# Modulation vectors as dot products along the rows, and small transfers on GpSimd's DMA queue

## The chip, the cores and the metric

One NeuronCore of one Trainium2 chip. The metric is device time in microseconds (us) from the first to the last instruction of one launch, with a little around it; the number given is the median of three runs. The engines are PE (TensorE matmul; PEld is its weight load), DVE (VectorE), ACT (ScalarE), POOL (GpSimd) and SP (SyncE). Each has its own instruction queue and runs it in order; SPq is SP's queue, which issues DMAs.

## The reference

Two transformer stacks on 256 tokens of width 1024, batch 1. The first has four layers of three sublayers each (SwiGLU, a mixer, SwiGLU); every sublayer is modulated by three vectors made from one conditioning row `c`:

```python
cond = silu(c)                                              # (1, 1024)
for i in range(4):
    mod = (cond @ w_mod[i] + b_mod[i]).reshape(-1, 3, 3, 1024)   # 9 vectors of 1024 for each layer
    ...
def _sublayer(x, fn, mod_j, g, b, weight):
    shift, scale, gate = mod_j[:, 0, None, :], mod_j[:, 1, None, :], mod_j[:, 2, None, :]
    y = fn(x * (1 + scale) + shift)
    return _layernorm(ALPHA * x + weight * gate * y, g, b)
```

The mixers are MLA attention (layers 0 and 3), differential attention (layer 1) and Mamba-2 (layer 2). The second stack is one block: a hybrid of dilated attention and retention, cross-attention to a memory of 256 tokens, and a SwiGLU. All is float32.

## The kernel before

Tokens lie in two tiles of 128 partitions (t = 0, 1). Each matrix product is done three times in a 12-bit split (high x high, high x low, low x high), so every weight tile that arrives is cast on ACT to its high part (`whi`, L219) and subtracted on DVE to its low part (`wlo`, L222). Weights come in pieces of 1 MB by SP's DMA queue into three buffers (`raw`, pool `rawp`), which the modulation weights share (`rawm`). The high and low parts live in a pool of `NW` = 21 buffers of 4 KB a partition.

A feed-forward sublayer (`ffn`, L598) has 11 blocks of 256 hidden units; a block is 48 matmuls of 512 columns into `hid` and 24 into `y`, with four transposes of `ac` between them. The mixers have hand-written step orders (`ORDER_MLA` and so on).

Work for later sublayers runs as background generators (`self.bg`): `tick` advances one by one step, at each block of an ffn (its `steps` argument spreads 32, 26 or 19 steps over the blocks) and at each "." of a mixer's order; `drain` runs what is left before the sublayer's result is normalized. The background makes the modulation vectors, each from four pieces of 1 MB:

- `mod_acc` (L357) loads a piece with the 1024 inputs over partitions and chunks and the 1024 outputs along the row, and adds up `acc[p, n]` over the eight chunks on DVE, with `cond` as a scalar of each partition. What remains is a sum over the 128 partitions.
- `mod_cols` (L375; 24 vectors, shift and scale) turns `acc` with eight 128x128 transposes on PE and sums each in a `tensor_reduce` on DVE, so that the vector comes out with features on partitions.
- `gate_row` (L410; 12 vectors) needs the vector as a row in all partitions (`gw`): it loads the bias broadcast, splits `acc` into high and low parts (ACT, DVE), and multiplies both halves with a matrix of ones on PE, four matmuls of 512 columns.

`post_ln` (L521) multiplies the sublayer's result by `gw`, then uses the rows `lng` and `lnb`. All DMAs, small ones too, are issued by SP.

The program is recorded in this order and then put in a queue for each engine by a list scheduler with a cost model; so an instruction's place in its queue is set before it runs, and it waits there for what it reads.

## Time and profile before

| | us |
|---|---|
| median of 3 runs (range) | 2570.22 (2568.35 to 2571.57) |
| the profiled execution, its span | 2567.9 |
| PE busy | 2497.5 |
| DVE busy | 2129.1 |
| ACT busy | 1286.9 |
| DMA, mean rate | 233 GB/s |

Only the span of the profiled execution is given (its own time with what lies around it is not); it is 2.3 us under the median of the three runs. Busy time counts a matmul until its modelled end, and matmuls overlap, so it is the distance from start to start that tells how fast PE goes through them.

### The profile page before, as it was taken

How to read it: one execution, taken by the hardware profiler on the slowest of the kernel's cores; microseconds unless marked ns; L12 is line 12 of the kernel's file. 1: busy time of each engine (PE TensorE's matmuls, PEld its weight loads, DVE VectorE, ACT ScalarE, POOL GpSimd, SP SyncE). 2: the span in 40 equal slices, each digit the busy share in tenths (PEclk: the TensorE clock that was granted, in tenths of full speed). 3: DMA queues.
4: the chain of work that ended last, by engine and by line, in shares of the span. 5: the costliest groups of instructions: out<-in, count | busy, mean ns of one | idle time of the engine just before them, and what ended most of it. 6: DMA issues, size and time to landing. Idle time of an engine off the chain costs nothing.

```text
span 2567.9 us, 34087 instructions
## 1 busy us (share of the span) xinstructions
PE 2497.5 (97%) x12252; PEld 2065.0 (80%) x12252; DVE 2129.1 (83%) x4847; ACT 1286.9 (50%) x2005; POOL 0.2 (0%) x4
## 2 busy tenths in 40 slices
PE   7999899999999999999999999999989999999998
PEld 6788688888887788888889778887878888788887
DVE  7888988879898988898989987698898856896754
ACT  3544474444446544544566554454446544555542
POOL 0000000000000000000000000000000000000000
PEclk9999999999999999999999999999999999999999
DMA  8888457848876388688742457658845754444552
GB/s 309 308 340 306 159 194 276 309 169 300 321 267 256 123 299 320 221 299 316 270 158 99 164 202 292 252 211 324 310 166 211 275 179 175 164 157 172 200 180 80
DMA packets 92297, 599.15 MB, mean 233 GB/s; under 512 B 12768, under 2 KB 14432, under 8 KB 24672
## 3 DMA queue, kind: packets, MB, share of 16 engines
q1 hardware_dynamic: 92128, 596.98, 63.5%
q8 instruction: 96, 1.57, 0.2%
q14 instruction: 73, 0.60, 0.1%
HBM read 593.79 MB, written 3.15 MB: 232 GB/s over the span
## 4 chain that ended last, share of the span: by engine, by line
PE 86%; DVE 7%; DMA 3%; ACT 2%; issue 1%; SPq 0%; DVEq 0%; ACTq 0%
PE tr L263 4%; PE y0q L640 3%; PE y0q L642 3%; PE y0q L641 3%; PE y1q L640 3%; PE y1q L642 3%; PE y1q L641 3%; DVE wlo L222 2%; PE hid0t L254 1%; PE hid6t L253 1%; PE hid9t L252 1%; PE hid6t L254 1%; PE hid9t L254 1%; PE hid6t L252 1%; PE hid5t L254 1%; PE hid9t L253 1%
## 5 line engine op out<-in xcount | busy, mean ns | idle before, releaser
L222 DVE TENSOR_TENSOR wlo<-raw,whi 128x384 fp32r<-128x384 f32 (+1 forms) x2385 | 1081.7, 505 | 145.8 <-ACT whi L219 76.0
L219 ACT ACTIVATE whi<-raw 128x1024 fp32r<-128x1024 f32 (+1 forms) x801 | 820.2, 1051 | 377.3 <-DMA raw<-in_ffn_w_in_dram 133.5
L371 DVE SCALAR_TENSOR_TENSOR acc<-rawm,cond,acc 128x1024 f32<-128x1024 f32 x252 | 322.9, 1281 | 13.2 <-DMA rawm<-in_w_mod_dram 8.0
L640 PE MATMUL y1q<-whi,ah 128*128 128x512 f32 x396 | 161.7, 408 | 1.7 <-ACT ah L625 1.7
L640 PE MATMUL y0q<-whi,ah 128*128 128x512 f32 x396 | 156.2, 394 | 0.7 <-ACT ah L625 0.2
L642 PE MATMUL y1q<-whi,al 128*128 128x512 f32 x396 | 156.4, 395 | 0.0
L641 PE MATMUL y0q<-wlo,ah 128*128 128x512 f32 x396 | 155.2, 392 | 0.0
L642 PE MATMUL y0q<-whi,al 128*128 128x512 f32 x396 | 155.2, 393 | 0.0
L641 PE MATMUL y1q<-wlo,ah 128*128 128x512 f32 x396 | 155.0, 391 | 0.0
L625 ACT ACTIVATE ah<-tr 128x256 fp32r<-128x256 f32 x198 | 74.7, 382 | 139.6 <-PE tr L263 136.7
L626 DVE TENSOR_TENSOR al<-tr,ah 128x256 fp32r<-128x256 f32 x198 | 82.0, 418 | 34.5 <-ACT ah L625 33.9
L640 PEld LDWEIGHTS y0q<-whi,ah 128*128 128x128 f32 x396 | 74.4, 188 | 17.1 <-ACT ah L625 2.6
L642 PEld LDWEIGHTS y1q<-whi,al 128*128 128x128 f32 x396 | 74.4, 188 | 15.7
L640 PEld LDWEIGHTS y1q<-whi,ah 128*128 128x128 f32 x396 | 74.5, 188 | 14.8 <-ACT ah L625 2.4
L642 PEld LDWEIGHTS y0q<-whi,al 128*128 128x128 f32 x396 | 74.3, 188 | 14.9 <-DVE al L626 0.2
L641 PEld LDWEIGHTS y0q<-wlo,ah 128*128 128x128 f32 x396 | 74.4, 188 | 14.5
L641 PEld LDWEIGHTS y1q<-wlo,ah 128*128 128x128 f32 x396 | 74.7, 189 | 13.2
L285 ACT ACTIVATE ev<-tr,B,G 128x128 f32<-128x128 f32 x192 | 72.9, 466 | 20.4 <-PE tr L263 20.3
L263 PEld LDWEIGHTS tr<-k_ident,ac 128*128 128x128 f32 x396 | 54.0, 140 | 29.6 <-DVE ac L616 3.0
L263 PE MATMUL tr<-k_ident,ac 128*128 128x128 f32 x396 | 74.5, 273 | 2.5 <-DVE ac L616 2.0
L295 DVE TENSOR_TENSOR tmp<-ev,tmp 128x512 fp32r<-128x512 f32 (+1 forms) x76 | 50.5, 664 | 12.7 <-ACT tmp L287 11.8
L252 PE MATMUL hid0t<-whi,tmp 128*128 128x512 f32 x144 | 56.4, 392 | 1.9 <-ACT tmp L287 1.9
(510 smaller groups left out, 6006.0 us busy)
## 6 DMA issues: line engine op xcount, KB each, us to landing
raw<-in_ffn_w_in_dram SPq DMA_DIRECT2D x176, 1024.0 KB, 4.9
rawm<-in_w_mod_dram SPq DMA_DIRECT2D x144, 1024.0 KB, 4.8
raw<-in_ffn_w_out_dram SPq DMA_DIRECT2D x88, 1024.0 KB, 5.0
raw<-in_w_gate_up_dram SPq DMA_DIRECT2D x22, 1024.0 KB, 4.7
raw<-in_w_in_dram SPq DMA_DIRECT2D x14, 1024.0 KB, 4.7
raw<-in_diff_w_in_dram SPq DMA_DIRECT2D x12, 1024.0 KB, 4.7
raw<-in_w_down_dram SPq DMA_DIRECT2D x11, 1024.0 KB, 4.7
raw<-in_w_kv_mem_dram SPq DMA_DIRECT2D x8, 1024.0 KB, 6.4
```

The source lines that it names most:

```text
L219: nc.scalar.activation(hi[:, q:e], s[:, q:e], AF.Copy)
L222: nc.vector.tensor_tensor(lo[:, q:e], s[:, q:e], hi[:, q:e].bitcast(F32), OP.subtract)
L252: nc.tensor.matmul(ps, xh, hi[:, off:off + n], start=first, stop=False)
L254: nc.tensor.matmul(ps, xl, hi[:, off:off + n], start=False, stop=last)
L263: self.nc.tensor.transpose(ps[:, j, :], src[:, j * P:(j + 1) * P], self.ident)
L285: nc.scalar.activation(src[:, j, :], ps[:, j, :], AF.Identity, scale=sc, bias=bcols[:, c + j:c + j + 1])
L371: nc.vector.scalar_tensor_tensor(o, src, sc, o, OP.mult, OP.add)
L625: nc.scalar.activation(ah, tr, AF.Copy)
L626: nc.vector.tensor_tensor(al, tr, ah.bitcast(F32), OP.subtract)
L640: nc.tensor.matmul(y[t][q], ah[:, k, :], hi[:, sl], start=f, stop=False)
L641: nc.tensor.matmul(y[t][q], ah[:, k, :], lo[:, sl], start=False, stop=False)
L642: nc.tensor.matmul(y[t][q], al[:, k, :], hi[:, sl], start=False, stop=l)
```

## The change

`w_mod` is laid out the other way: outputs on partitions, inputs along the row. `silu(c)` is kept as a row in all partitions (`condrow`, 4 KB a partition, for which `NW` goes from 21 to 20). A vector is then eight `scalar_tensor_tensor` instructions that multiply 1024 weights by `condrow` and add up along the row into one column of `pv` (`accum_out`); the product itself is written over the weights. Shift and scale are done with that. A gate is transposed once on PE (8x128), copied by ACT to `gs`, written to DRAM and read back broadcast to all partitions. The last two, and nearly all small transfers, go by GpSimd's queue. The number of background steps for each vector falls, and so do the ffn's `steps`.

```diff
-NR, NW, NT, NH = 3, 21, 12, 10
+NR, NW, NT, NH = 3, 20, 12, 10
...
     def bcast_row(self, dst, src, n):
         ap = bass.AP(tensor=src.tensor, offset=src.offset, ap=[[0, P], [1, n]])
-        self.nc.sync.dma_start(dst, ap)
+        self.nc.gpsimd.dma_start(dst, ap)
...
-    def mod_acc(self, i, s, m):
+    def mod_dot(self, i, s, m, pv):
         nc = self.nc
-        acc = self.tmp([P, 1024], name="acc")
         for u in range(4):
             raw = self.rawp.tile([P, 2048], F32, tag="raw", name=self.nm("rawm"))
             nc.sync.dma_start(raw, self.A["w_mod"][i, s * 3 + m, u])
             for j in range(2):
-                k = 2 * u + j
-                sc = self.cond[:, k:k + 1]
-                for q in range(0, 1024, ACH):
-                    src, o = raw[:, j * 1024 + q:j * 1024 + q + ACH], acc[:, q:q + ACH]
-                    if k == 0:
-                        nc.vector.tensor_scalar(o, src, sc, None, op0=OP.mult)
-                    else:
-                        nc.vector.scalar_tensor_tensor(o, src, sc, o, OP.mult, OP.add)
+                src = raw[:, j * 1024:(j + 1) * 1024]
+                nc.vector.scalar_tensor_tensor(src, src, 1.0, self.condrow, OP.mult, OP.mult,
+                                               accum_out=pv[:, 2 * u + j:2 * u + j + 1])
             yield
...
     def mod_cols(self, i, s, m):
         nc = self.nc
-        yield from self.mod_acc(i, s, m)
-        acc = self.acc
-        yield
         pv = self.small(8, "pv")
-        for a in range(0, 8, 4):
-            ps = self.transposes(acc[:, a * P:(a + 4) * P], 4)
-            nc.vector.tensor_reduce(pv[:, a:a + 4], ps, axis=AX.X, op=OP.add)
+        yield from self.mod_dot(i, s, m, pv)
...
     def gate_row(self, i, s):
         nc = self.nc
-        yield from self.mod_acc(i, s, 2)
-        acc = self.acc
+        pv = self.small(8, "pv")
+        yield from self.mod_dot(i, s, 2, pv)
+        nc.vector.tensor_tensor(pv, pv, self.bias_cols(i, s, 2), OP.add)
+        ps = self.bank("tr", "mod")
+        nc.tensor.transpose(ps[:8, :P], pv, self.ident)
+        gs = self.half([8, P], name="gs")
+        nc.scalar.activation(gs, ps[:8, :P], AF.Copy)
+        row = self.dr.tile([8, P], F32, name=self.nm("grow"))
+        nc.gpsimd.dma_start(row, gs)
         gw = self.tmp([P, D], name="gw")
-        self.bcast_row(gw, self.A["b_mod"][i, (s * 3 + 2) * D:(s * 3 + 3) * D], D)
-        for q in range(2):
-            sl = slice(q * 512, (q + 1) * 512)
-            ah, al = self.half([P, 512], F32R, "ah"), self.half([P, 512], F32R, "al")
-            nc.scalar.activation(ah, acc[:, sl], AF.Copy)
-            nc.vector.tensor_tensor(al, acc[:, sl], ah.bitcast(F32), OP.subtract)
-            yield
-            ps = self.bank("tr", "mod")
-            nc.tensor.matmul(ps, self.ones, ah, start=True, stop=False)
-            nc.tensor.matmul(ps, self.ones, al, start=False, stop=True)
-            nc.vector.tensor_tensor(gw[:, sl], ps, gw[:, sl], OP.add)
+        nc.gpsimd.dma_start(gw, row.rearrange("(o a) p -> o (a p)", o=1).to_broadcast([P, D]))
         self.gates[i, s] = gw
         yield
...
-        self.cond = c.tile([P, 8], F32, name="cond")
-        nc.scalar.activation(self.cond, cT, AF.Silu)
+        self.condrow = c.tile([P, D], F32, name="condrow")
+        self.bcast_row(self.condrow, A["crow"], D)
+        nc.scalar.activation(self.condrow, self.condrow, AF.Silu)
...
-                    self.ffn(xc, A["ffn_w_in"][f], A["ffn_w_out"][f], done, 32 if s == 0 else 26 if i + 1 in EARLY else 19)
+                    self.ffn(xc, A["ffn_w_in"][f], A["ffn_w_out"][f], done, 26 if s == 0 else 21 if i + 1 in EARLY else 16)
...
-    w = v["w_mod"].reshape(DEPTH, 4, 2, P, 9, D)
-    A["w_mod"] = np.ascontiguousarray(w.transpose(0, 4, 1, 3, 2, 5)).reshape(DEPTH, 9, 4, P, 2048)
+    A["crow"] = v["c"].reshape(D)
+    w = v["w_mod"].reshape(DEPTH, D, 9, 4, 2, P)
+    A["w_mod"] = np.ascontiguousarray(w.transpose(0, 2, 3, 5, 4, 1)).reshape(DEPTH, 9, 4, P, 2048)
```

Beside these, `nc.sync.dma_start` becomes `nc.gpsimd.dma_start` for the constants of `setup_late`, the positions and frequencies, `subg`, the Mamba constants, the writes of the memory's keys and values (`mk`, `mv`) and their reads in `cross` (`xk`, `xv`), the tables of `hybrid` and three norm gains: 89 DMAs in all leave by GpSimd's queue, and every 1 MB weight piece stays on SP's.

The schedule of each engine moves with it. On PE, in the first ffn, a shift or scale vector stood between the last `hid` matmul of block 3 and the first `y` matmul (`tr` is a PSUM bank, `acc` the sums):

```order
L252 MATMUL hid3t_225_1274<-whi_1209,tmp_608 128x512
L253 MATMUL hid3t_225_1274<-wlo_1210,tmp_608 128x512
L254 MATMUL hid3t_225_1274<-whi_1209,tmp_610 128x512
L263 MATMUL tr_1304<-k_ident,acc_1107 128x128 x4
L263 MATMUL tr_1310<-k_ident,acc_1107 128x128 x4
L640 MATMUL y1q_164_962<-whi_1013,ah_1183 128x512
L641 MATMUL y1q_164_962<-wlo_1014,ah_1183 128x512
```

After, the same place has only the two transposes of the block's own hidden units (`ac`):

```order
L252 MATMUL hid3t_218_1243<-whi_1178,tmp_577 128x512
L253 MATMUL hid3t_218_1243<-wlo_1179,tmp_577 128x512
L254 MATMUL hid3t_218_1243<-whi_1178,tmp_579 128x512
L263 MATMUL tr_1283<-k_ident,ac_1225 128x128 x2
L625 MATMUL y1q_157_931<-whi_982,ah_1152 128x512
L626 MATMUL y1q_157_931<-wlo_983,ah_1152 128x512
```

The eight transposes of `acc` are gone; nothing of the modulation stands on PE there. ACT's queue at the start of the kernel, before (`m`: the memory's tokens, `raw`: the first weights, `tmp` and `ev`: the memory's transposed tokens):

```order
L456 ACT_TABLE_LOAD
L456 ACTIVATE cond<-k_cT 128x8
L1143 ACTIVATE msq_103,ss_105<-m_85 128x1024
L1143 ACTIVATE msq_104,ss_106<-m_87 128x1024
L219 ACTIVATE whi_177<-raw_175 128x1024
L292 ACTIVATE tmp_99<-ev_142 128x4x128
```

And after:

```order
L445 ACT_TABLE_LOAD
L445 ACTIVATE condrow<-condrow 128x1024
L1128 ACTIVATE msq_98,ss_100<-m_83 128x1024
L1128 ACTIVATE msq_99,ss_101<-m_85 128x1024
L937 ACT_TABLE_LOAD
L937 ACTIVATE alog_11667<-alog_11667 128x32
L219 ACTIVATE whi_172<-raw_170 128x1024
L292 ACTIVATE tmp_94<-ev_137 128x4x128
```

The activation of the 1024 wide row `condrow` now stands ahead of the squares of the memory, and Mamba's `alog`, whose data come by GpSimd's queue, ahead of the first weight cast. That queue begins like this after (it had no DMA before):

```order
L332 DMA condrow<-in_crow_dram 128x1024
L1398 DMA pre_mix_g_690<-in_pre_mix_g_dram 128x8
L1398 DMA pre_mem_g_692<-in_pre_mem_g_dram 128x8
L1398 DMA pre_ffn_g_694<-in_pre_ffn_g_dram 128x8
L460 DMA k_tri<-in_tri_dram 128x128
L460 DMA k_slow<-in_slow_dram 128x128
L460 DMA k_ln_gT<-in_ln_gT_dram 128x96
L460 DMA k_ln_bT<-in_ln_bT_dram 128x96
L460 DMA k_mla_norm_g<-in_mla_norm_g_dram 128x10
L479 DMA posi<-in_positions_dram 128x2
L861 DMA subg<-in_diff_subln_g_dram 128x1
L332 DMA alog_11667<-in_ssm_a_log_dram 128x32
```

`posi` is the tenth DMA of that queue and `alog` the twelfth; `posi` and `subg` are read by DVE in the middle of the memory's first normalization (after `rv` of the second token tile).

## Rows read from the trace of the kernel before

**Rows 1.** Stretches: length, busy time and count by engine, PE clock, DMA share, GB/s.

```profile
20.00:45.00 25.00, 24.36 (x199) 23.69 (x198) 18.26 (x28) 8.10 (x10) 0.00 (x0) 0.99 0.95 365
...
1080.00:1275.00 195.00, 194.43 (x898) 159.28 (x897) 176.04 (x349) 88.39 (x132) 0.00 (x0) 1.00 0.80 296
1275.00:1490.00 215.00, 206.64 (x1337) 183.52 (x1336) 190.98 (x549) 128.02 (x183) 0.00 (x0) 0.98 0.38 134
```

**Rows 2.** PE's waits from 78 to 270 us: us, times, longest.

```profile
PE tr L263 <- DVE ac L616: 0.9, 1, 0.9
```

**Rows 3.** Timeline of PE at a shift or scale vector: start, us, what, count.

```profile
138.28 0.40 PE L254 MATMUL hid3t<-whi,tmp 128*128 128x512 f32 x1
138.52 1.04 PE L263 MATMUL tr<-k_ident,acc 128*128 128x128 f32 x8
139.31 0.48 PE L640 MATMUL y1q<-whi,ah 128*128 128x512 f32 x1
139.63 0.40 PE L641 MATMUL y1q<-wlo,ah 128*128 128x512 f32 x1
139.86 0.39 PE L642 MATMUL y1q<-whi,al 128*128 128x512 f32 x1
```

**Rows 4.** Timeline of PE at a gate: its first matmul, and the one after it.

```profile
190.78 0.39 PE L423 MATMUL mod<-ah,ones 128*128 128x512 f32 x1
...
191.71 0.39 PE L640 MATMUL y1q<-whi,ah 128*128 128x512 f32 x1
```

**Rows 5.** Groups by line: names, shapes, count, busy us, mean ns, idle before.

```profile
L371 DVE SCALAR_TENSOR_TENSOR acc<-rawm,cond,acc 128x1024 f32<-128x1024 f32 x252 | 322.9, 1281 | 13.2 <-DMA rawm<-in_w_mod_dram 8.0
...
L383 DVE TENSOR_REDUCE pv<-tr 128x4 f32<-128x512 f32 x48 | 31.2, 682 | 8.4 <-PE tr L263 8.4
...
L369 DVE TENSOR_SCALAR acc<-rawm,cond 128x1024 f32<-128x1024 f32 x36 | 26.9, 746 | 1.2 <-DMA rawm<-in_w_mod_dram 0.9
...
L425 DVE TENSOR_TENSOR gw<-mod,gw 128x512 f32<-128x512 f32 x24 | 16.3, 681 | 6.0 <-PE mod L424 6.0
L420 DVE TENSOR_TENSOR al<-acc,ah 128x512 fp32r<-128x512 f32 x24 | 16.2, 687 | 4.4 <-ACT ah L419 4.4
...
L574 ACT ACTIVATION_READ_ACCUMULATOR sq<-x 128x1 f32 x12 | 2.4, 200 | 0.0
```

**Rows 6.** Timeline of DVE in the first ffn: four multiply-adds in a row.

```profile
238.82 5.24 DVE L371 SCALAR_TENSOR_TENSOR acc<-rawm,cond,acc 128x1024 f32<-128x1024 f32 x4
```

**Rows 7.** Timeline of SP's queue: the first two DMA issues.

```profile
0.73 0.39 SPq L443 DMA_DIRECT2D k_cT<-in_cT_dram  x1
1.18 0.42 SPq L443 DMA_DIRECT2D k_ident<-in_ident_dram  x1
```

**Rows 8.** Tiles lnb (issue times, min/median/max) and gw (landing times).

```profile
L332 SPq DMA_DIRECT2D lnb<-in_ln_b_dram x12: 328/422/1425, 185.0 to 2039.5; - x12
...
DMA to landing us min/median/max: 3.4/5.8/8.2
```

**Rows 9.** DMA issues: count, KB each, us from issue to landing.

```profile
posi<-in_positions_dram SPq DMA_DIRECT2D x1, 1.0 KB, 3.9
alog<-in_ssm_a_log_dram SPq DMA_DIRECT2D x1, 16.0 KB, 5.3
```

**Rows 10.** Timelines of ACT, DVE and PE in the start stage.

```profile
5.78 1.06 ACT L1143 ACTIVATE msq<-m 128x1024 f32<-128x1024 f32 x1 [3.17 <-DMA m<-in_mem_dram]
...
11.16 1.06 ACT L219 ACTIVATE whi<-raw 128x1024 fp32r<-128x1024 f32 x1 [2.89 <-DMA raw<-in_w_kv_mem_dram]
...
8.31 0.15 DVE L314 TENSOR_SCALAR rv<-ss 128x1 f32<-128x1 f32 x1
...
70.56 0.73 PE L252 MATMUL pmv<-whi,tmp 128*128 128x512 f32 x2 [2.54 <-ACT whi L219]
```

**Rows 11.** Groups of ACT from 1275 to 1490 us, one table load of Mamba's.

```profile
L975 ACT ACT_TABLE_LOAD x1 | 1.3, 1283 | 0.0
```

**Rows 12.** Tile gw in the first MLA stage (270 to 392 us).

```profile
L425 DVE TENSOR_TENSOR gw<-mod,gw x2: 683/688/692, 352.9 to 362.8; 128x512 f32<-128x512 f32 x2
L528 DVE SCALAR_TENSOR_TENSOR r<-y0q,gw x2: 680/686/692, 358.3 to 363.5; 128x512 f32<-128x512 f32 x2
```

More of the change, by code (lines that the diff above doesn't have):

```diff
@@ L363, in mod_acc, with bias_cols @@
             for j in range(2):
-                k = 2 * u + j
-                sc = self.cond[:, k:k + 1]
-                for q in range(0, 1024, ACH):
-                    src, o = raw[:, j * 1024 + q:j * 1024 + q + ACH], acc[:, q:q + ACH]
-                    if k == 0:
-                        nc.vector.tensor_scalar(o, src, sc, None, op0=OP.mult)
-                    else:
-                        nc.vector.scalar_tensor_tensor(o, src, sc, o, OP.mult, OP.add)
+                src = raw[:, j * 1024:(j + 1) * 1024]
+                nc.vector.scalar_tensor_tensor(src, src, 1.0, self.condrow, OP.mult, OP.mult,
+                                               accum_out=pv[:, 2 * u + j:2 * u + j + 1])
             yield
-        self.acc = acc
+    def bias_cols(self, i, s, m):
+        o = (i * 9 + s * 3 + m) * 8
+        return self.bmod[:, o:o + 8]
     def mod_cols(self, i, s, m):
         nc = self.nc
-        yield from self.mod_acc(i, s, m)
-        acc = self.acc
-        yield
         pv = self.small(8, "pv")
-        for a in range(0, 8, 4):
-            ps = self.transposes(acc[:, a * P:(a + 4) * P], 4)
-            nc.vector.tensor_reduce(pv[:, a:a + 4], ps, axis=AX.X, op=OP.add)
-        b = self.bmod[:, (i * 9 + s * 3 + m) * 8:(i * 9 + s * 3 + m + 1) * 8]
+        yield from self.mod_dot(i, s, m, pv)
+        b = self.bias_cols(i, s, m)
         k = i * 3 + s - 1
@@ L454, in setup @@
         self.bmod = const("b_modT", [P, 288])
-        self.cond = c.tile([P, 8], F32, name="cond")
-        nc.scalar.activation(self.cond, cT, AF.Silu)
-        self.ones = c.tile([P, P], F32R, name="ones")
-        onesf = self.half([P, P], name="onesf")
-        nc.vector.memset(onesf, 1.0)
-        nc.vector.tensor_copy(self.ones, onesf)
+        self.condrow = c.tile([P, D], F32, name="condrow")
+        self.bcast_row(self.condrow, A["crow"], D)
+        nc.scalar.activation(self.condrow, self.condrow, AF.Silu)
     def setup_x(self):
@@ L956, in mamba @@
         cw = self.cst.tile([P, 24, 4], F32, name="cw")
-        nc.sync.dma_start(cw, A["ssm_conv_w"])
+        nc.gpsimd.dma_start(cw, A["ssm_conv_w"])
         cbb = self.cst.tile([P, 24], F32, name="cbb")
-        nc.sync.dma_start(cbb, A["ssm_conv_b"])
+        nc.gpsimd.dma_start(cbb, A["ssm_conv_b"])
         ng = self.cst.tile([P, 16], F32, name="ng")
-        nc.sync.dma_start(ng, A["ssm_norm_g"])
+        nc.gpsimd.dma_start(ng, A["ssm_norm_g"])
         dt, dta, ea, w, z, ys = {}, {}, {}, {}, {}, []
@@ L1205, in hybrid @@
                 K[name] = h[:, o:o + n]
[L1206 removed]
+                nc.gpsimd.dma_start(K[name], A[name])
                 o += n
         dec = self.tmp([P, 4, 256], name="dec")
[L1209 removed]
+        nc.gpsimd.dma_start(dec, A["decay"].rearrange("p (a b) -> p a b", a=4))
         db = self.half([P, P])
[L1211 removed]
+        nc.gpsimd.dma_start(db, A["dbias"])
         dbias = c.tile([P, P], BF16, name="dbias_b")
@@ L1412, in run @@
             g2[n] = self.cst.tile([P, 8], F32, name=n)
-            nc.sync.dma_start(g2[n], A[n])
+            nc.gpsimd.dma_start(g2[n], A[n])
         def grow(name):
```

27 lines of the change are left out of this document (11 added, 16 removed).

## The prediction

> **What bounds the kernel now.** I read the stretches by stage first. In an ffn with five modulation vectors (1080 to 1275 us) PE is busy 194.4 of 195 us, DVE 176.0, ACT 88.4, and the DMA engines 80% of the time at 296 GB/s [rows 1]. Then PE's waits: over the whole first ffn the longest line is 0.9 us [rows 2]. So in the ffns, which are most of the time, PE ends everything, and a PE instruction that disappears gives back its slot. Busy time is not the slot, since matmuls overlap: from start to start a matmul of 512 columns takes 139.86 - 139.63 = 0.23 us, not its 0.40 [rows 3]. Only the start stage and the first steps of each mixer are different: there PE waits for DVE and ACT, and what stands in front in their queues decides.
>
> **What leaves PE.** A shift or scale vector takes eight transposes: 139.31 - 138.52 = 0.79 us to the next matmul's start. That matmul then holds its slot 0.32 us (139.63 - 139.31) instead of 0.23, since its weight load is not hidden, and so the vector costs 0.79 + 0.09 = 0.88 us [rows 3]. 24 vectors: 21.1 us. A gate takes four matmuls from 190.78 to 191.71, 0.93 us [rows 4]; 12 gates: 11.2 us. What comes is one transpose for a gate: 0.79 / 8 = 0.10 us plus at most the 0.09, so 1.2 to 2.3 us for 12; I take 1.6. Net: 21.1 + 11.2 - 1.6 = 30.7 us off PE. Nearly all of it lies in ffns where PE is the bound; two vectors lie in the start stage and three gates in mixers (6 x 0.9 = under 5 us, of which part may have lain in PE's waits). I count 30.7 and put up to 3 us of doubt on it.
>
> **DVE.** Before, a vector was one first product and seven multiply-adds, 0.746 + 7 x 1.281 = 9.71 us; shift and scale add two sums over transposes (2 x 0.682, together 11.08), a gate two subtractions and two additions (2 x 0.687 + 2 x 0.681, together 12.45) [rows 5]. In all 24 x 11.08 + 12 x 12.45 = 415 us. After, it is 288 products with a sum along the row and twelve additions of eight columns, which I leave out. No row of before shows a DVE instruction with an accumulator. From below: the present ones stand 5.24 / 4 = 1.31 us apart, each reading the sum that the one before it wrote [rows 6]; the new ones need not wait for each other, so a product with its sum may come out at or somewhat under 1.28. From above: on ACT an accumulator's read is an instruction of its own of 0.200 us [rows 5]. I take 1.281 + 0.1: 288 x 1.38 = 398 us, 17 us less than before; with 0.2 it would be 427, 12 us more. Since DVE has 19 us to spare in the fullest ffn [rows 1], this is worth nothing by itself; PE hides it. The cover goes only if a product takes far longer (first rival).
>
> **ACT, the weight buffers and the steps.** 24 casts and the split leave ACT, which is idle half of the time. `NW` falls from 21 to 20: ten pairs of high and low parts stay, what goes is the one cast that ACT could make ahead of its partner, 1.06 us [rows 10], covered by ACT's idle half in an ffn; uncovered, it would be that 1.06 us for an ffn. In Mamba's stage ACT gets two more table loads (an `alog`-like change of table among Silu and Exp), 1.28 us each [rows 11]; ACT is busy 128 of 215 us there and PE 206.6 [rows 1], so I take 0.5 of the 2.6 us. The vector steps fall from 6 or 7 to 5, and the `steps` numbers with them, so the work is spread over the same blocks.
>
> **SP's queue** loses the small issues, and no longer waits for a buffer of `lng` or `gw` with weight pieces behind it. But PE hardly waits for weights in the ffns [rows 2]; I count nothing.
>
> **The start, where the change adds waits.** GpSimd issued no DMA before, so its issue is bounded by SP's: 1.18 - 0.73 = 0.45 us from issue to issue [rows 7], and 1.43 us for the longest issue [rows 8]. No row is nearer to the one or the other, so I take the middle, 0.95. (a) `condrow` is a 512 KB broadcast like `gw`, which lands 3.4 to 8.2 us after issue, median 5.8 [rows 8]: at 0.73 + 5.8 = 6.5, and its activation (1.06) holds ACT until 7.6, while the squares of the memory, queued behind it, began at 5.78 [rows 10]: 1.8 us lost (0 to 4.2). (b) DVE's cast of `posi`, the tenth issue, stands among the small steps after 8.31 [rows 10]: 0.73 + 9 x 0.95 + 3.9 [rows 9] = 13.2, against 8.4 + 1.8 = 10.2, so 3.0 more (0 to 7.3). (c) `alog`, the twelfth, stands ahead of the first weight cast, which began at 11.16 [rows 10]: 0.73 + 11 x 0.95 + 5.3 = 16.5 [rows 9], 5.4 late (0 to 10.6). (b) and (c) run side by side; the later counts: 5.4. Against that: shift and scale of the first sublayer are ready without PE and without the sums, so that the first inputs are scaled while PE still makes the memory's values, and ACT's weight casts no longer come late for PE, which waited 2.54 us for one [rows 10]. With two smaller ones of that kind I take 3.5 us back (0 to 4.7). Net at the start: +1.9 us, between -4 and +11.
>
> A rule bears on (a) to (c). The row: no small transfer lands under 3.9 us, and `condrow`'s like takes 5.8 [rows 8, 9]. The Trainium skill (DMA: Bandwidth & Descriptors, Anatomy of one DMA) has a fixed 2.0 us plus the bytes at 436 GB/s for a DMA from this queue, and little for making descriptors; by it `condrow` would land 3.2 us after issue, nothing would wait, and the sum would be some 5 us lower. No run here shows it yet.
>
> **The gate's detour.** In a mixer a gate used to be ready just in time: in the first MLA its second half was added at 362.8, and used from 363.5 [rows 12]. Now it is done two steps sooner (steps lie 362.8 - 352.9 = 9.9 us apart), at about 343, but then goes through two DMAs: 2 x (0.95 + 5.8) = 13.5, so 356.5, against a first use at 358.3 [rows 12]. It holds by 2 us; at the longest landing of 8.2 [rows 8] it comes 3 us late, in three mixers. I take 0, and up to 9 us in the range.
>
> **The sum,** against this execution's span of 2567.9: - 30.7 (PE) + 0.5 (tables) + 1.9 (start) = 2539.6. The median of the runs stands 2.3 above the span, so 2541.9. PE's few waits for the sums over transposes go too (1 to 2 us, not in the rows): 2540.
>
> **Rivals.**
> 1. *DVE becomes the bound, and the kernel slower.* If a product with its sum ran at half rate, 2.56 us: without modulation the ffn from 1080 has 176.0 - 4 x 11.08 - 12.45 = 119 us of DVE work; 40 products at 2.56 make it 221 against 195 before. Four such ffns: + 105 us, less what the rest gains (some 12): 2660. It decides from a product of 1.98 us on, where 4 x (119 + 40 x 1.98 - 195) eats the other 13 us. For it: no row shows the instruction. Against: with the same operands it now takes 1.28 [rows 5].
> 2. *The start and the gates cost more.* At 1.43 us an issue the start loses 10.6 - 3.5 = 7 instead of 1.9, and late gates add up to 9: 2546 to 2554. A mechanism that would bring it about: descriptors made in software while DVE, at work nine tenths of an ffn, holds them up. The Trainium skill (SBUF — State Buffer, Who interferes with whom) has this rule: DVE's fast two-port copies and scalar operations lock GpSimd out of its SBUF port. The change removes 36 such candidates (the 0.746 us products, against 1.28 for two inputs [rows 5]), which speaks for little of it.
> 3. *PE's time goes into waits for weights; no gain.* With 4.5 us less for an ffn the DMA rate has to rise from 296 to 303 GB/s; 365 GB/s are reached from 20 to 45 us [rows 1]. So against it. Time: about 2570.
> 4. *The start gains.* If GpSimd's small transfers land quickly, nothing is lost there and 3.5 to 4.7 is won, and the ffns lose their small stalls too: 2530 to 2535.
>
> **How the numbers follow.** Forecast with the start within its bounds (2533 to 2546): 0.60. Rival 4: 0.13. Rival 2: 0.15. Rival 3, or a new order of the queues that eats the gain: 0.06. Rival 1, or any other loss of that size: 0.06. The range takes the forecast with the bounds of the start, of the gates and of the tables, so rivals 2 and 4 with it: 2528 to 2556. About 0.2%, 5 us, is what a measurement of this kernel can tell from no change. Faster: 0.60 + 0.13 + 0.15 = 0.88; same 0.06; slower 0.06.
>
> **What would show it.** PE: no `tr` from `acc`, no `mod` of 512 columns; ffns of the first stack some 4 us (five vectors) to 3 us (three) shorter. DVE: `scalar_tensor_tensor` near 1.28 us with an accumulator read under 0.2; over 1.7 us, the forecast falls. Start: ACT's wait before `alog` and DVE's before `posi`, GpSimd's issues 0.5 to 1.4 us apart, the first ffn's first matmul moved by -4 to +11 us. Mixers: no wait of DVE for `gw`. PE waits growing in the ffns by tens of us would prove rival 3.

## The result: 0.65% slower, and where the time is in the profile after

| | kernel before | changed kernel |
|---|---|---|
| median of four runs (range), us (of the kernel before, the three ahead and one more) | 2569.28 (2565.57 to 2571.57) | 2584.62 (2575.30 to 2589.02) |
| ratio to the kernel before, 95% interval | | 1.0065 (1.0044 to 1.0085) |
| span of the profiled execution, us | 2567.9 | 2573.4 |
| mean granted clock of PE | 0.992 | 0.989 |
| PE busy, DVE busy, us | 2497.5, 2129.1 | 2475.2, 2072.1 |

The prediction was 2540 us, in a range of 2528 to 2556, with a chance of 0.88 for faster. The changed kernel is slower. Run again beside the experiments, it took 2580.73 us where the kernel before took 2566.95 (ratio 1.0055, interval 1.0038 to 1.0072). The profiled execution was the fastest of the four, so what the trace shows (5.5 us) is the smaller part of the loss of 15.3.

I cut both traces at the first matmul of each stage and compared stage by stage. First the ffns whose modulation changed, of the changed kernel: the first row has four vectors (two shifts or scales, two gates), the second five (four and one), as the ffn in [rows 1], the third three (two and one); the last line sums all eight ffns. Columns: stretch, length, busy time and count of PE, PE's weight loads, DVE, ACT and POOL, granted clock, share of the DMA engines, GB/s.

```profile
898.90:1087.60 188.70, 188.23 (x854) 153.71 (x854) 158.23 (x358) 91.45 (x134) 3.16 (x6) 1.00 0.78 284
1087.60:1277.60 190.00, 188.80 (x855) 153.95 (x854) 167.27 (x376) 88.79 (x134) 3.16 (x6) 1.00 0.82 301
...
388.40:577.20 188.80, 188.20 (x854) 153.88 (x852) 148.61 (x338) 90.72 (x132) 2.10 (x4) 1.00 0.72 256
...
sum 1519.30, PE 1506.98 PEld 1230.35 DVE 1247.45 ACT 718.98 POOL 25.48; mean PE 188.37 PEld 153.79 DVE 155.93 ACT 89.87 POOL 3.19
```

The same three ffns, and the same sum, of the kernel before:

```profile
884.40:1077.30 192.90, 192.36 (x876) 157.01 (x877) 166.05 (x336) 94.11 (x138) 0.00 (x0) 1.00 0.76 279
1077.30:1270.50 193.20, 192.77 (x889) 157.84 (x888) 174.24 (x347) 89.19 (x134) 0.00 (x0) 1.00 0.79 296
...
377.20:568.30 191.10, 190.47 (x873) 156.44 (x872) 154.02 (x321) 92.20 (x134) 0.00 (x0) 1.00 0.69 253
...
sum 1542.20, PE 1532.26 PEld 1255.12 DVE 1301.85 ACT 729.38 POOL 0.00; mean PE 191.53 PEld 156.89 DVE 162.73 ACT 91.17 POOL 0.00
```

So the ffns did much of what was forecast: 4.2 us less with four vectors, 3.2 with five, 2.3 with three, and 22.9 us less in all. The four ffns with five vectors are uneven: 5.0, 0.5, 3.2 and 4.8 us less. Now the start, the first MLA, diff, Mamba and the second MLA of the changed kernel:

```profile
0.00:89.60 89.60, 59.87 (x321) 51.76 (x322) 59.65 (x142) 41.27 (x61) 12.80 (x27) 0.92 0.78 289
279.50:388.40 108.90, 94.89 (x518) 79.24 (x518) 90.05 (x236) 59.55 (x123) 2.11 (x4) 0.95 0.49 173
770.00:898.90 128.90, 121.70 (x619) 96.00 (x618) 107.08 (x274) 72.24 (x150) 2.10 (x4) 0.96 0.49 177
1277.60:1505.00 227.40, 217.51 (x1384) 191.82 (x1383) 201.11 (x566) 135.93 (x195) 0.00 (x0) 0.98 0.40 139
1885.30:1992.80 107.50, 94.72 (x519) 79.04 (x519) 89.99 (x236) 59.34 (x123) 2.10 (x4) 0.97 0.50 175
```

and of the kernel before:

```profile
0.00:78.40 78.40, 58.82 (x337) 51.25 (x338) 57.91 (x115) 36.40 (x57) 0.20 (x4) 0.93 0.82 310
273.30:377.20 103.90, 95.97 (x520) 79.90 (x521) 91.73 (x231) 61.03 (x125) 0.00 (x0) 0.97 0.51 182
761.60:884.40 122.80, 117.98 (x621) 93.60 (x619) 108.69 (x269) 71.77 (x150) 0.00 (x0) 1.00 0.51 185
1270.50:1496.00 225.50, 216.99 (x1386) 191.90 (x1385) 201.48 (x567) 135.09 (x199) 0.00 (x0) 0.98 0.40 141
1883.60:1987.90 104.30, 96.23 (x521) 80.31 (x522) 90.87 (x229) 60.07 (x124) 0.00 (x0) 0.97 0.50 180
```

The start is 11.2 us longer, the first MLA 5.0, diff 6.1, Mamba 1.9, the second MLA 3.2. Together that is 27.4 us, more than the ffns give. The clock column is part of it: a stretch's length times (1 - clock) is the most that PE can have lost at its lower level, since time in which it waits anyway counts in it. By these rows that is 16.2 us before (5.5, 3.1, 0, 4.5, 3.1) and 25.5 us after (7.2, 5.4, 5.2, 4.5, 3.2), 9.3 us more. The columns of PE say the same from the other side: the time in which PE is not busy grew by 24.7 us in these stages, and its busy time by 2.7, although by the prediction's prices some 4.2 us of its work had gone from them. So the clock's part is some 7 us, an estimate, and at most 9.3 by these rounded rows; most of the loss is PE's waits.

**The start.** Rows of ACT, of DVE, of SP's queue and of PE in the changed kernel, each engine for itself in order of time; a bracket says how long the engine stood idle before and what ended that.

```profile
7.59 1.06 ACT L445 ACTIVATE condrow<-condrow 128x1024 f32<-128x1024 f32 x1 [5.58 <-DMA condrow<-in_crow_dram]
8.56 1.04 ACT L1128 ACTIVATE msq<-m 128x1024 f32<-128x1024 f32 x1
...
15.74 0.23 ACT L937 ACTIVATE alog<-alog 128x32 f32<-128x32 f32 x1 [3.71 <-DMA alog<-in_ssm_a_log_dram]
15.88 1.04 ACT L219 ACTIVATE whi<-raw 128x1024 fp32r<-128x1024 f32 x1
...
13.82 0.17 DVE L481 CAST posf<-posi 128x2 f32<-128x2 int32 x1 [2.77 <-DMA posi<-in_positions_dram]
...
31.88 12.45 SPq L361 DMA_DIRECT2D rawm<-in_w_mod_dram  x4
46.57 3.02 SPq L211 DMA_DIRECT2D raw<-in_w_kv_mem_dram  x2
...
54.02 0.73 PE L252 MATMUL pmv<-whi,tmp 128*128 128x512 f32 x2 [4.57 <-ACT whi L219]
...
74.62 1.22 PE L252 MATMUL pmv<-whi,tmp 128*128 128x512 f32 x2 [7.08 <-ACT whi L219]
```

The squares, the cast of `posi` and the first weight cast are late as in [rows 10] against these: 5.78 became 8.56, and 11.16 became 15.88. But two waits have grown as well. Four pieces of vector rows stand in SP's queue ahead of the third weights of the memory (issued at 46.57; in the kernel before two stood there, and these weights were issued at 37.57), and PE waits 4.57 us for them. In the kernel before it waited here too, but less:

```profile
47.56 0.57 PE L253 MATMUL pmv<-wlo,tmp 128*128 128x512 f32 x1 [3.09 <-DVE wlo L222]
```

Then ACT scales the first inputs before it casts the fourth weights, and PE waits 7.08 us, where [rows 10] has 2.54.

**The opening of the first MLA.** DVE in the changed kernel; `rs` and `rt` are the steps of the root that PE's next transposes (of `cn`) need:

```profile
289.72 0.21 DVE L320 TENSOR_SCALAR rs<-rt,rs 128x1 f32<-128x1 f32 x1
289.84 1.21 DVE L364 SCALAR_TENSOR_TENSOR rawm<-rawm,condrow 128x1024 f32<-128x1024 f32 x1
...
290.98 0.27 DVE L319 TENSOR_SCALAR rt<-rh,rs 128x1 f32<-128x1 f32 x1
291.17 1.22 DVE L364 SCALAR_TENSOR_TENSOR rawm<-rawm,condrow 128x1024 f32<-128x1024 f32 x1
...
292.62 0.48 DVE L753 TENSOR_SCALAR cn<-pa,rs 128x256 f32<-128x256 f32 x1
...
295.05 1.23 DVE L364 SCALAR_TENSOR_TENSOR rawm<-rawm,condrow 128x1024 f32<-128x1024 f32 x1 [1.46 <-DMA rawm<-in_w_mod_dram]
```

Two products stand in the middle of that chain; in the kernel before the first piece of the vector came on DVE only after it, at 296.2 (there the chain's end was at 284.51). It is in the order of the instructions, and could have been seen before the run. PE waits 5.53 us there, where the kernel before has 3.67. Then the third product stands ahead of the last step of `kr` (296.20), which PE transposes next; it waits 1.46 us for its own rows to land and takes 1.2, and PE waits a second time, 2.60 us. Over the whole execution PE's line for this wait (put down to `rv`, the step behind) was `0.6, 1, 0.6` (us, times, longest) before and is now

```profile
PE tr L263 <- DVE rv L314: 4.1, 2, 2.6
```

What these two waits grew by is 4.5 of the 5.0 us of the first MLA. At the opening of diff three products stand in such a chain (777.77 to 781.63), and PE waits 3.17 us, where the longest wait there was 1.21.

What the clock does behind these openings, first in the MLA, then during and behind the wait in diff (stretches of the changed kernel, columns as above):

```profile
293.00:297.00 4.00, 1.24 (x4) 0.63 (x5) 2.54 (x15) 0.18 (x1) 0.00 (x0) 0.50 0.59 202
...
781.00:785.00 4.00, 0.83 (x5) 0.39 (x4) 4.00 (x8) 2.60 (x3) 0.00 (x0) 1.00 1.00 414
785.00:790.00 5.00, 4.25 (x17) 3.28 (x17) 5.00 (x9) 4.38 (x11) 0.00 (x0) 0.52 0.38 161
```

The clock falls to its lower level of 1.2 GHz (0.50 and, with some time at the upper level, 0.52). In the MLA PE is in its second wait for most of that stretch, so little is lost in it; in diff it is busy 4.25 of 5 us again, and works at half speed.

### The profile page after: what moved, and what is told of

It is laid out like the page before. It is cut to its first block, busy times and chain, and to the rows that moved or that the text cites. A ratio compares the mean times of both kernels' runs of the same rounds, so it can differ in the third digit from the quotient of the medians.

```text
span 2573.4 us, 34066 instructions
## 1 busy us (share of the span) xinstructions
PE 2475.2 (96%) x12024; PEld 2041.0 (79%) x12024; DVE 2072.1 (81%) x5049; ACT 1281.1 (50%) x1995; POOL 47.8 (2%) x93
## 4 chain that ended last, share of the span: by engine, by line
PE 81%; DVE 10%; DMA 4%; ACT 4%; issue 2%; DVEq 0%; POOL 0%; ACTq 0%; SPq 0%; POOLq 0%
DVE wlo L222 3%; PE tr L263 3%; PE y0q L625 3%; PE y0q L627 3%; PE y0q L626 3%; PE y1q L625 3%; PE y1q L626 3%; PE y1q L627 3%; DMA rawm<-in_w_mod_dram 2%; PE hid9t L252 1%; PE hid8t L253 1%; PE hid9t L254 1%; PE hid2t L252 1%; PE hid4t L252 1%; PE hid4t L254 1%
## 5 line engine op out<-in xcount | busy, mean ns | idle before, releaser
L364 DVE SCALAR_TENSOR_TENSOR rawm<-rawm,condrow 128x1024 f32<-128x1024 f32 x288 | 342.3, 1222 | 27.5 <-DMA rawm<-in_w_mod_dram 26.7
L626 PEld LDWEIGHTS y1q<-wlo,ah 128*128 128x128 f32 x396 | 74.7, 189 | 13.2
L295 DVE TENSOR_TENSOR tmp<-ev,tmp 128x512 fp32r<-128x512 f32 (+1 forms) x76 | 50.9, 670 | 17.8 <-ACT tmp L287 16.6
```

Source lines behind the costliest of these rows:

```text
L364: nc.vector.scalar_tensor_tensor(src, src, 1.0, self.condrow, OP.mult, OP.mult, accum_out=pv[:, 2 * u + j:2 * u + j + 1])
L626: nc.tensor.matmul(y[t][q], ah[:, k, :], lo[:, sl], start=False, stop=False)
```

## The experiments

Times are medians; the ratio is to the kernel before, run on the same chip beside each group. The groups ran on different chips, so the ratios compare them, and a difference in us between groups is only about right. Theory A says that the loss is made by the order: products that stand in the chains which open a layer, and the vectors' rows ahead of the weights at the start. Theory B says that GpSimd's DMA queue makes everything late. Theory C came later: a wait of PE costs a second time, by the clock.

**The changed kernel again, as the reference.**

> The changed kernel itself, beside the three that follow, as their reference on the same chip. If its loss belongs to the kernel and not to one chip: ratio to the kernel before 1.0065 within its interval of 1.0044 to 1.0085, so 2580 to 2589 where the kernel before takes 2567 to 2569. If it comes out at 2576, the three runs that came to 2576 gained nothing.

2580.73 us, ratio 1.0055 (1.0038 to 1.0072). The loss belongs to the kernel. So a run below that comes to 2576 has gained 4 to 5 us, not 8 to 9. The intervals of the runs hold, start_held, dots_sp and start_sp_b overlap this one, so what each of these four gained is read from its stages; those of the other runs on the changed kernel lie clear of it. In the trace of this run (span 2582.8) the loss is larger than in the first: the ffns sum to 1525.6 us, only 16.6 less than before, and the start is 13.2 us longer.

**Products behind the chain.**

```diff
+                with self.tc.issue_after(self.mark):
                     nc.vector.scalar_tensor_tensor(src, src, 1.0, self.condrow, OP.mult, OP.mult, ...
```

> The changed kernel with one edge: no modulation product is placed on DVE ahead of the last transposed half of the layer's input. In the two MLAs and in diff that puts the products back behind the short root-of-variance chain that PE waits for; everything else stays. Theory A (products in the chains, and the start): MLA0 back from 108.9 to about 104 us, diff from 128.8 to 123, MLA1 from 107.5 to 104.5, so 12 to 14 us less than the changed kernel's median of 2584.6: about 2572, ratio to the kernel before about 1.001. Theory B (the second DMA queue is slow everywhere): the chains are not the cause, the time stays at 2584.

2575.78 us, ratio 1.0039 (1.0023 to 1.0055). Diff came back as forecast, to 123.6 us. The MLAs did not: 109.4 and 110.2 us. (The traced execution took 2581.04 us, 5 over the median.) The wait at the opening fell from 5.53 to 3.50 us (3.67 in the kernel before), and the second one of 2.60 is gone, but new ones came at the query projections; PE, SP's queue and DVE in this run:

```profile
313.99 0.47 PE L252 MATMUL pq<-whi,tmp 128*128 128x512 f32 x1 [2.16 <-DVE vt L793]
317.48 0.80 PE L253 MATMUL pq<-wlo,tmp 128*128 128x512 f32 x1 [3.03 <-DVE wlo L222]
...
305.59 2.43 SPq L211 DMA_DIRECT2D raw<-in_mla_w_q_dram  x2
...
313.94 1.22 DVE L365 SCALAR_TENSOR_TENSOR rawm<-rawm,condrow 128x1024 f32<-128x1024 f32 x1
...
316.88 1.36 DVE L222 TENSOR_TENSOR wlo<-raw,whi 128x384 fp32r<-128x384 f32 x3
```

The rows already stood in two of the three raw buffers, and stayed there until the products were done (the second began at 304.33, its sum was read at 305.48), so the query weights were issued at 305.59 instead of 292.42. That alone is not the cause: the kernel before issued them at 298.73, 25 us into its stage as here 26, and its waits at this place were 1.19 and 0.37 us. What differs is the place of the next two products: they stand from 313.94 to 316.35 ahead of the `wlo` that PE waits 3.03 us for. So the edit freed one short chain, and the products came to stand in the next.

**The start's order put right, GpSimd's queue kept.**

```diff
-        nc.scalar.activation(self.condrow, self.condrow, AF.Silu)
...
+        with self.tc.issue_after(squares):
+            nc.scalar.activation(self.condrow, self.condrow, AF.Silu)
...
+        with self.tc.issue_after(self.mark_d):
             nc.vector.tensor_copy(pf, pi)
...
+        with self.tc.issue_after(self.mark_a):
             nc.scalar.activation(alog, alog, AF.Exp)
```

> The changed kernel with the start's order put right and nothing else: Silu of condrow behind both squares of the memory on ACT, the casts of posi and subg behind the memory's last transposed half on DVE, alog's Exp behind the memory's values on ACT. All transfers stay on GpSimd's queue. Theory A: PE's first matmul back from 15.6 to about 10 us, so 5.6 us less than the changed kernel: about 2579; PE's wait of 7 us for the last weights of the memory's values (ACT scales the first inputs before them) stays. Theory B: as little as 0 to 2 us less, because the queue itself delays what follows.

2575.96 us, ratio 1.0036 (1.0023 to 1.0049). PE's first matmul came at 11.53 us instead of 15.56, and the first ffn at 84.6 instead of 89.6, so 5.0 of the 11.2 us are this order. The waits for the third and fourth weights stayed, at 6.88 (4.57 in the changed kernel) and 6.51 us.

**All small transfers on SP's queue again.**

```diff
-        nc.gpsimd.dma_start(row, gs)
+        nc.sync.dma_start(row, gs)
```

(and so at all twenty places)

> The changed kernel with all its small transfers on SP's queue again, gate rows too; the row products stay. Products in the chains of MLA and diff stand where they stand in the changed kernel. Theory A: only the start changes, since the scheduler then puts posi, subg and alog late: 5 to 8 us less than the changed kernel, 2577 to 2580. Theory B (the queue): all that was lost comes back, 2545 or less.

2576.73 us, ratio 1.0041 (1.0025 to 1.0056). The first ffn starts at 83.2 us; the first MLA still takes 110.3 and diff 128.2. Theory B falls: without GpSimd's queue only the start gets better. PE's first matmul is back at 9.38 us there, and its waits for the third and fourth weights are still 7.81 and 6.51 us.

**The queue alone, on the kernel before.**

```diff
-        self.nc.sync.dma_start(dst, ap)
+        self.nc.gpsimd.dma_start(dst, ap)
```

(and so at all small transfers)

> The kernel before with its small transfers on GpSimd's queue (constants, rows, the memory's keys and values out and in, lng, lnb, gw) and nothing else: modulation by multiply-add, sums over transposes, gates by the matrix of ones. Theory A: the start loses 3 to 5 us by posi and alog, the rest nothing: 2573, ratio 1.0015. Theory B: most of the loss of 45 us against the sum of the parts is here: 2585 or more.

2573.65 us, ratio 1.0026 (1.0017 to 1.0035): 6.6 us more, where theory A had 3 to 5 and theory B 18 or more. The start accounts for them: the first ffn comes at 85.2 us instead of 78.4. The other stages are 3.2 us shorter to 2.3 us longer, with no sign of theory B's 18.

**Another order at the start.**

```diff
-L0 . . L1 . K0 . . . . K1 L2 . R . . V2 X Q E0 E1 L3 V3
+L0 . . L1 K0 . L2 . K1 . L3 . R . . V2 X . . . Q E0 E1 V3
```

(with the one-time transfers on SP's queue)

> The changed kernel with another start: the one-time transfers (condrow, constants, Mamba's parameters) on SP's queue, and the start's order with its modulation steps later, so that the third and fourth weights of the memory are loaded ahead of the last vectors' rows, and cast ahead of the first inputs' scaling. Theory A (fewer steps for a vector under an unchanged list of ticks pull its loads ahead of the weights): PE's waits for those weights, 4.6 and 7.1 us in the changed kernel, fall to under 3 together, PE's first matmul comes back to about 10 us, and the first ffn starts at 73 to 78 us instead of 89.6: 11 to 15 us less than the changed kernel. Rival (the start is bound by its 18 MB of transfers): the ffn starts no earlier than 80, 5 to 8 us less, as by the start's queue alone.

2577.28 us, ratio 1.0044 (1.0029 to 1.0059). PE's waits for the memory's weights are gone, but the time is not; PE in this run:

```profile
64.92 0.39 PE L254 MATMUL pmv<-whi,tmp 128*128 128x512 f32 x1
79.83 0.80 PE L252 MATMUL hid0t<-whi,tmp 128*128 128x512 f32 x1 [14.52 <-ACT whi L219]
```

PE is done with the memory at 65 us and then waits 14.5 us, since the second vector is complete only at 70, ACT scales the first inputs from then until 78, and casts the ffn's weights behind that. The rival of this run, that the ffn starts no earlier than 80, came closest: the wait moved to the end. That it is the transfers which set that end is not shown; in this order it is the second vector, whose rows now come after the weights. The 79.8 us are still 3.4 less than the 83.2 with all small transfers on SP's queue and the old order.

**Gates of the middle layers made in the ffn ahead.**

```diff
-EARLY = (2,)
+EARLY = (1, 2, 3)
...
+                    if i == 0:
+                        self.bg.append(self.gate_row(0, 1))
```

> The changed kernel with the gates of all four middle layers made in the ffn ahead of them (only Mamba's was), so that no modulation product is left in MLA0, diff and MLA1, and each of three ffns has one vector more. Start as in the changed kernel. Theory A (products in the chains that open a layer): MLA0 108.9 to 103, diff 128.8 to 121, MLA1 107.5 to 103, together 16 to 18 us; the three ffns get 0 to 2 us longer each, so 12 to 16 us less than the changed kernel. Rival (what is lost in the layers is the removed PE work that stood in waits, and the tables): 5 us less at most.

2570.79 us, ratio 1.0014 (1.0001 to 1.0028): 9.9 us less than the changed kernel. The first ffn, which now has six vectors, the first MLA, diff, and an ffn that went from three vectors to four (the second of layer 2) in this run:

```profile
88.40:292.20 203.80, 192.68 (x847) 154.41 (x845) 172.64 (x396) 88.65 (x127) 3.86 (x7) 0.98 0.85 313
292.20:392.00 99.80, 94.68 (x516) 80.14 (x517) 78.91 (x213) 57.13 (x121) 1.04 (x2) 0.97 0.38 133
773.90:896.40 122.50, 118.48 (x618) 92.90 (x616) 98.07 (x257) 71.84 (x149) 0.00 (x0) 1.00 0.40 140
...
1502.47:1694.22 191.75, 189.01 (x857) 153.89 (x855) 156.03 (x357) 90.46 (x134) 3.14 (x6) 1.00 0.75 276
```

Without products the layers take 99.8, 122.5 and (the second MLA) 101.5 us, so the gate's work, loads and products together, costs 9.1, 6.4 and 6.0 us there. A fourth vector costs an ffn of three 0.1 us (188.9 against 188.8, the second of layer 0) and some 2.5 us (191.75 against 189.2, layer 2), and the first ffn gives 13.9 us back: six vectors are too many for it.

**Both.**

> Both: the other start and the gates out of the layers. If the two losses are separate, the gains add: 24 to 30 us less than the changed kernel, so about 2556 and some 11 us under the kernel before (ratio about 0.995). If both are made by one thing (the queues or the clock as a whole), it is no better than the better one of the two.

2565.53 us, ratio 1.0002 (0.9987 to 1.0017). The two gains add (3.5 and 9.9 alone, 15.2 together), but are smaller than expected, each for the reason just shown.

**Work added where PE waits.**

```diff
+    def fill(self, x, t, ws, n, count):
+        ps = self.bank("tr", "fill")
+        with self.tc.issue_after(self.last_mm):
+            for j in range(count):
+                hi, lo, off = ws[j % len(ws)]
+                self.nc.tensor.matmul(ps[:, :n], x.h.at(j % len(ws), t), hi[:, off:off + n], start=True, stop=True)
```

> The changed kernel with work added: while PE waits at the opening of each MLA it repeats 24 matmuls of 384 columns (4.1 us), and at the opening of diff 12 of 512 columns (2.7 us), into a bank that nobody reads. No wait of another engine changes. Theory C (a wait of PE costs twice, once itself and once by the half clock that follows it): the clock no longer falls there, the time lost to it (by the profile of the changed kernel 5.4 us in MLA0, 3.2 in MLA1, 5.2 in diff) shrinks by 5 to 9 us in all, and the kernel is faster by that with more work on PE: 2572 to 2576 where the changed kernel takes 2581 to 2585. Rival (the waits alone cost, the clock follows something else): the same time, or some us more.

2571.86 us, ratio 1.0018 (1.0009 to 1.0028): some 8.9 us faster than the changed kernel with 60 more matmuls on PE. The first MLA, diff and the second MLA:

```profile
280.10:385.60 105.50, 97.03 (x542) 81.95 (x542) 89.78 (x236) 59.65 (x123) 2.10 (x4) 1.00 0.50 179
766.10:892.00 125.90, 120.61 (x631) 94.92 (x630) 106.90 (x274) 71.86 (x150) 2.10 (x4) 1.00 0.51 181
1879.20:1985.30 106.10, 97.84 (x543) 82.97 (x543) 89.68 (x236) 59.64 (x123) 2.10 (x4) 0.98 0.50 177
```

The clock stands at 1.00, 1.00 and 0.98 where it stood at 0.95, 0.96 and 0.97, and the stages are 3.4, 3.0 and 1.4 us shorter. The traced execution is the fastest of eleven, with a mean clock of 0.995; the other ten have 0.990 to 0.993, the nine of the changed kernel 0.986 to 0.989. Theory C holds, and diff is where it shows best: DVE's order at its opening is the same as in the changed kernel, the added matmuls fill all but 0.47 us of the wait of 3.17, and the clock stays at 1.00. In the MLAs the schedule moved as well: the third product now stands behind that step of `kr` (294.76 and 294.60 in the first), and PE's second wait fell from 2.60 to 0.71 us, so that up to 1.9 of the 3.4 us there are order and not clock.

**All of it together, first without the added work.**

```diff
+        yield
         b = self.bias_cols(i, s, m)
...
-EARLY = (2,)
+EARLY = (1, 2, 3)
...
-A0 B0 tA0 ? K00 K01 * V00 . A1 B1 tK00 tB0 tK01 tA1 V01 . Q00 Q02 . K10 tQ00 Q01 K11 tQ02 V10 tB1 tQ01 S00 V11
+A0 B0 tA0 ? K00 K01 * V00 A1 B1 tK00 tB0 tK01 tA1 V01 Q00 Q02 K10 tQ00 Q01 . K11 tQ02 . V10 tB1 tQ01 . S00 V11 .
```

(with the one-time transfers on SP's queue, and the ffns' `steps` at 30, 23 and 18)

> The changed kernel with all that the runs so far speak for: one-time transfers on SP's queue; a sixth step for each shift and scale vector, as before, so that the unchanged list of ticks at the start again lets the third weights in ahead of the second vector's last rows; the gates of diff and the second MLA made in the ffn ahead; in the first MLA the gate's steps behind the loads of the query weights. The row products stay everywhere. Theory A: start 78 to 80 us as before (83.2 with the queue alone), MLA0 103 to 105, diff 122, MLA1 102, ffns 188.7 to 193: about 2555, ratio to the kernel before 0.994 to 0.997. If the start stays at 83, the missing steps are not its cause; if the ffns with one vector more take over 2 us more each, the gain is given back there: 2565.

2565.19 us, ratio 0.9994 (0.9984 to 1.0005). The MLAs (102.2 and 101.8) and diff (122.5) came out as expected or better. The first MLA still makes its own gate, only with its steps later in the list, and is 6.7 us shorter than in the changed kernel: its waits at the opening are one of 3.5 us. So here it is the place of the gate's work that costs, and not the work. The start did not come out: 85.4 us. The sixth step let the third weights in sooner, and their wait fell to 3.18 us, but that for the fourth, whose casts stand behind the first inputs on ACT, grew to 11.07. So the missing steps move the wait, and are not its cause.

**And with it, and the fourth weights ahead of the first inputs.**

```diff
-L0 . . L1 . K0 . . . . K1 L2 . R . . V2 X Q E0 E1 L3 V3
+L0 . . L1 . K0 . . . . K1 L2 . R . . V2 X Q L3 E0 E1 V3
```

> The kernel of the run best1 with three edits: the fourth weights of the memory loaded and cast ahead of the scaling of the first inputs; 18 repeated matmuls of 384 columns (3.1 us) in PE's wait at the opening of each MLA; 14 repeated matmuls of 512 columns (3.2 us) after the memory's third block, where PE waits for the fourth's weights. Theory: the wait of 11.2 us before the fourth block falls to about 4, the first ffn starts at 77 to 80 us instead of 85.4, the clock's loss in the two MLAs (2.0 us each) and some of the 8.3 in the start goes: 10 to 14 us less than best1's 2565, so 2551 to 2555, ratio 0.994 to 0.996. Rival (the start is bound by its transfers): the ffn starts at 83 to 85 again, 2560.

2553.26 us, ratio 0.9949 (0.9932 to 0.9965): 14 us faster than the kernel before, and some 27 than the changed one. PE's wait for the fourth weights fell to 1.72 us. The start, the first MLA, diff, Mamba and the second MLA:

```profile
0.00:77.30 77.30, 59.23 (x335) 51.93 (x335) 52.91 (x118) 36.83 (x56) 2.10 (x7) 0.98 0.88 318
273.60:374.90 101.30, 95.89 (x537) 80.65 (x536) 90.31 (x239) 59.77 (x123) 2.13 (x4) 1.00 0.52 189
763.20:887.30 124.10, 119.81 (x617) 94.00 (x617) 98.07 (x257) 71.90 (x149) 0.00 (x0) 0.99 0.38 138
1268.10:1492.50 224.40, 214.47 (x1384) 189.39 (x1383) 201.13 (x566) 135.71 (x195) 0.00 (x0) 1.00 0.39 140
1874.90:1975.10 100.20, 95.49 (x535) 80.61 (x535) 80.94 (x219) 58.78 (x122) 1.07 (x2) 1.00 0.40 141
```

The start loses 1.5 us to the clock instead of 7.2, the MLAs nothing, and every one of these stages but diff is shorter than in the kernel before, 7.6 us in all. The eight ffns, which here make two gates more than in the changed kernel, sum to 1536.5 us: only 5.7 less than before, where the changed kernel had 22.9.

**The added work on the kernel before.**

> The kernel before with the same repeated matmuls at the openings of the MLAs and after the memory's third block, and nothing else. If the clock's fall after a wait is a property of the chip and not of the change, the kernel before gains too: its clock loses 3.1 us in each MLA and 5.0 in the start, so 4 to 7 us less, 2560 to 2563, ratio 0.9975. It then is what best3 has to be held against. If only the changed kernel's order makes the clock fall: the same time, or 1 to 3 us more.

2565.19 us, ratio 0.9993 (0.9984 to 1.0002). It gained only 2 us, not 4 to 7: the second MLA went from 104.3 to 102.3 us with a clock of 1.00, the first stayed at 104.0 with 0.97, and the start got 3 us longer. (The traced execution is the second slowest of eleven; nine of them show a mean clock of 0.995 or more, against seven of 21 of the kernel before.) So of the 14 us of the run before this, the added work alone would have given the old kernel 2. That the other 12 are due to the row products is not shown: the kernel before was not run with the gates made early and the new order of the start.

## Why the prediction was wrong, step by step

| stage | predicted, us | measured, us |
|---|---|---|
| start (1.9, less 1.8 for its two vectors on PE) | +0.1 | +11.2 |
| first MLA, diff, second MLA (a gate each) | -0.8 each | +5.0, +6.1, +3.2 |
| Mamba | +0.5 | +1.9 |
| eight ffns (22 vectors, 9 gates) | -26.5 | -22.9 |
| what follows | 0 | +1.0 |
| sum, against the span of 2567.9 | -28.3 | +5.5 |

- **What leaves PE: right.** 2.3 and 2.5 us off the ffns with three vectors against 2 x 0.88 + 0.8 = 2.6; 4.2 off the one with four against 2 x 0.88 + 2 x 0.8 = 3.4; on average 3.4 off those with five against 4 x 0.88 + 0.8 = 4.3. The ffns with fewer than five reach 188.7 to 189.2 us; those with five take 189.9, 192.8, 190.0 and 191.1. The one at 192.8 came out 3.8 us short of its forecast, as much as all eight together (3.6): its longest wait, 2.53 us, is for a cast of weights that were issued behind three pieces of vector rows in SP's queue. That is read from the trace and not tested.
- **DVE: right in sign, and cheaper than priced.** The group of the products in the changed kernel, from the tiles read on its line, and the count of their sums:

```profile
L364 DVE SCALAR_TENSOR_TENSOR rawm<-rawm,condrow x288: 1212/1222/1234, 27.1 to 2043.1; 128x1024 f32<-128x1024 f32 x144
L364 DVE DVE_READ_ACCUMULATOR rawm<-rawm,condrow x288: 80/84/97, 28.2 to 2044.2; 128x1 f32 x144
```

  From start to start a product and its read take 1.14 us (289.84 to 290.98), not 1.38, and DVE is busy 57 us less in all. The first rival, a product at half rate, is out.
- **The start: the listed delays were right, the gain set against them was the failed term.** The squares came 2.8 us late (1.8 predicted), `posi` was cast at 13.82 (13.2), `alog` taken at 15.74 (16.5), and PE's first matmul was 5.5 us late (5.4 was predicted for the first weight cast, which came 4.7 late). The issue was cheaper than thought, 0.54 us, but after eight issues the ninth waited 2.22 us for `condrow` to land. What failed is "I take 3.5 us back": vectors that are ready sooner were to help PE. Their loads took the queue slots of the third weights, and the scaling that they release took ACT ahead of the fourth, so 3.5 back became 5.7 more (11.2 less the 5.5 of the first matmul). The run with another order of the start, in which both waits are gone, bears this out in part: it took 3.4 us off the run with SP's queue and the old order. Of the 3.5, [rows 10] has 2.54; for the two smaller terms the prediction gave no row.
- **The transfers.** `condrow` was in use 6.3 us after its issue (1.25 to 7.59), near the 5.8 of [rows 8]. The Trainium skill's 2.0 us and bytes at 436 GB/s (DMA: Bandwidth & Descriptors, Anatomy of one DMA) would have had 3.2, an estimate; the measurement decides. GpSimd's issues in the trace of the changed kernel last 0.51 to 0.68 us, all 89 of them. So nothing is seen there of the Trainium skill's rule that DVE's copies hold GpSimd up (SBUF — State Buffer, Who interferes with whom); whether such a copy ran beside an issue is not shown.
- **The mixers: the step that failed is "I take 0" for the gate.** I priced the gate's two transfers, and these were harmless: in the first MLA the second of them was issued at 356.19 us and landed 4.3 us later, at 360.5, 9 us before the first use at 369.7. What the prediction left out is where the products go, though the prediction's first paragraph names the first steps of each mixer as the place where what stands in front in DVE's queue decides. Before, a vector's first piece needed a free accumulator tile; a product that writes onto its own input needs none, and was placed sooner, in the chain that PE waits for. That the tile was what held it back is my reading. That the place costs the time is shown by diff, which came back when the products alone were moved (128.9 to 123.6 us), by the first MLA, whose gate was only moved within it (108.9 to 102.2), and by all three layers without the gate (9.1, 6.4 and 6.0 us less). The prediction had "a new order of the queues that eats the gain" at 0.06, without a place or a price; the order of the instructions gave both.
- **No term for the clock.** At most 9.3 us of the loss, by the estimate above some 7, is time at the lower level, in diff right behind a wait that became longer. Mamba's 1.9 has none of that (0.98 before and after); its table loads rose from 13 to 15 in that stage, as forecast, and I did not separate them further.
- **The end of the range.** The forecast's chances put 0.06 on slower. The four layers, in which little was to change, came out 16.2 us longer, and that lay outside the sum.

## What to carry to other kernels

An instruction that loses an input or a scratch tile may also lose the wait that kept it out of the way: after such a change, look in the order of the instructions at each short chain that the bound engine waits for, and at what now stands in it. Weights and vector rows share three buffers and one queue, so work that comes sooner comes at the expense of something else, and a wait that is taken away at one place can come back at the next, as it did in the first MLA and twice in the start. And a longer wait of PE can cost a second time, by the clock behind it.

## What the runs showed of the hardware

- A single wait of PE can cost twice. At the opening of diff the longest wait is 1.21 us in the kernel before, with a clock of 1.00 behind it, and 3.17 us in the changed kernel, with 0.52 over 5 us. Of the traces of all runs, the five with a wait of 3.16 to 3.56 us there show the lower level in the next 5 us, and the nine with 1.08 to 1.21 do not. But the length of one wait does not decide it: later in that stage the changed kernel waits 1.83 us and the clock falls (0.72 over the next 6 us), its second trace waits 1.82 and filler 1.83 at that place, both with 1.00 behind it, and best3 waits 1.16 with 0.66 over the next 5 us. What else decides is open.
- So it can pay to keep PE busy with matmuls that nobody reads: with 60 of them the three stages they stand in were 7.8 us shorter (a part of it by the changed order in the MLAs), and the changed kernel some 8.9 us faster. On the kernel before, whose waits are shorter, 50 gave 2 us, with an interval that includes 1.
- DVE sums a product along the row at no visible price: 1.22 us for 1024 columns and 0.08 us for the read, 1.14 us from start to start, against 1.28 us for the multiply-add of [rows 5], which stands 1.31 apart in [rows 6].
- The executions of one kernel with row products lie up to 22 us apart in one run (2546 to 2568 in best3), those of the kernel before 11 us at most. What makes that spread stays open.
